# In the last layer, q's swaps asked for earlier, value products two steps later, and the q norms' scale folded into their power

## The chip, the cores and the metric

The kernel runs on one core of one Trainium2 chip. The metric is device microseconds for one execution of the whole program. A core has five engines, each with its own instruction queue: PE (TensorE, matrix products, with PEld for its weight loads), DVE (VectorE), ACT (ScalarE), POOL (GpSimd) and SP (SyncE, which here only issues DMAs). An engine runs its instructions in the order of its queue; a wait for another engine, or for a DMA, stops everything behind it in that queue.

## The reference

The program is a two-layer encoder over 272 tokens (16 learned meta tokens and 256 inputs), 2048 wide, in fp32. Each layer has an attention branch and a Fourier branch, then a gated convolution network. The part on which the change acts:

```python
proj = rmsnorm(h) @ w_in                       # q | k | v | f | ga | gf
q = rope_2d(rmsnorm(q, q_norm))                # 8 heads of 128
k = rope_2d(rmsnorm(k, k_norm))                # 2 heads, each shared by 4 q heads
p = softmax(q @ k.T / sqrt(128))
attn = p @ v
fr = Re(fft2(f over tokens and 128 channels))  # per channel group
h = h + (sigmoid(ga) * (attn @ w_attn_br) + sigmoid(gf) * (fr @ w_four)) @ w_out
```

After the second layer the meta tokens are dropped.

## The kernel before

**Products.** Every fp32 product is made from high and low parts. Weights come as chunks of 128x1024 (512 KB), loaded by SP (`load_raw`, L264) into a ring of four `raw` buffers (a few more in some stages). ACT casts a chunk to its high part (`wh`, L306), and DVE subtracts that to get the low part (`wl`, L308). Three matmuls then make one product: `wh` with the input's high part (L377), `wh` with its low part (L378), `wl` with the high part (L379). A `raw` buffer comes free when its `wl` is made, and SP issues the next load into it then, in its own order. In the last layer the products of q and of the gates are 258 columns wide, since 14 of the meta tokens are needed only as keys.

**Steps.** While such a product is under way, the smaller work of attention runs in its shadow. That work is written as generators (`kstats` for the k norm and rope, `vtrans`, `q_stage` for a pair of q heads, `attend` and `attention`, `folded_chan`), pushed onto a list with a number of steps to wait. After every second pair of weight block and output half, `group` calls `step()` (one step of the first generator that is due; `yield n` means that it waits n steps) and `pump()` (one split of the next chunk). This order of writing is what the scheduler starts from. It then orders each engine's instructions by its own estimate, except where `keep_in_program_order` or `manual_schedule` fixes them.

**Last layer.** The order is k, v, q0, q1, then `folded_f` (the Fourier product over 16 chunks of a folded weight `fw`, chunk numbers 448 to 463, whose matmuls are L869 and L872 with the high part and L873 with the low part `wl`), q2, q3, then gates (`ga`, `gf`) and branch products. q1 and `folded_f` are under `manual_schedule` for DVE, and the end of q1 and `folded_f` for ACT too.

**q_stage.** `head_evac` (L926 to L937) brings a pair of heads out of PSUM: ACT squares (L935), DVE scales (L936) into `qp`. `swap` (L946 to L950) is four DMAs on SP that exchange 32-row blocks of `qp` into `qs`, for rope. `rope` (L952 to L958) then multiplies `qs` (L953) and `qp` (L954), adds (L955), casts to the high part (ACT, L956) and subtracts to the low part (L958), all but the cast on DVE. The q norms: the sums of squares go through PE (L943) and DVE (L944, L1050, L1054), L1055 turns the 9 sums `qv` into mean plus epsilon, and POOL raises them to the power -1/2 (L518, in `pow_half`), which gives `rq`. `attention` begins by multiplying `rq` by 1/sqrt(128) on DVE (L1074).

**attention.** For each of two kv heads there are nine items: the meta tokens of four heads, then four heads by two blocks of 128 queries. An item goes through `scores` (PE L1094 to L1096 into `ps_s`; DVE maximum L1098 and bias L1100; ACT exponential L1103), `normalise` (DVE L1108 to L1112 into `pn`), `transposed` (PE L1120 into `ps_pt`; ACT L1133 writes the high part PH, DVE L1134 the low part PL and L1136). Once both blocks of a head are transposed, `values` (L1138 to L1146) makes seven matmuls into `ps_pv`: twice L1141 (PH), L1142 (PL), L1143 (PH), and one L1144. In every turn of the loop the values of the head that was finished stand behind `transposed` of a later item. PH and PL are one tile each for all four heads.

Of the kernel before, what the change touches and what calls it, by code (L numbers as in the profile page):

```python
# [13 lines left out]
ALU = mybir.AluOpType  # L14
# [9 lines left out]
HD = 128  # L24
# [5 lines left out]
EPS = 1e-6  # L30
# [131 lines left out]
def encoder_kernel(ctx, tc, xT, params, consts, bmat, cfold, csign, w_fl, w_f64c, w_in, w_abr, w_four, w_f64, w_out, w_up, w_down, w_vn, w_dn, w_dt, out):  # L162
    nc = tc.nc
# [150 lines left out]
    def push(gen, wait=0):  # L314
        shadow.append([wait, gen])
# [20 lines left out]
    def until(hold, flag):  # L336
        while flag not in hold:
            step(True)
# [174 lines left out]
    def bc2(ap):  # L513
        return _rep(ap, 2)

    def pow_half(out, src):
        n = src.shape[1]
        nc.gpsimd.tensor_tensor(out, src, mhalf[:, :n], op=ALU.pow)  # L518
# [115 lines left out]
    for l in range(DEPTH):  # L634
        last = l == DEPTH - 1
# [6 lines left out]
        with tc.tile_pool(name=f"mix{l}", bufs=1) as mp:  # L642
# [17 lines left out]
            def rt(name):  # L660
                return mp.tile([P, 2, 2 * TH], F32, tag="r", name=name, bufs=7)[:, :, :T]
# [4 lines left out]
            def ut(name):  # L666
                return mp.tile([P, T], F32, tag="u", name=name, bufs=2)
# [271 lines left out]
            def sums_t(dst, blocks):  # L939
                n = len(blocks)  # L940
                ss = psum.tile([P, 512], F32, tag="aux", name="ps_ss")
                for i in range(n):
                    nc.tensor.transpose(ss[:, i * P:(i + 1) * P], blocks[i], ident)  # L943
                nc.vector.tensor_reduce(dst, ss[:, 0:n * P].rearrange("p (i n) -> p i n", i=n), axis=AX.X, op=ALU.add)  # L944

            def swap(hp):  # L946
                qs = rt("qs")
                for b in range(4):
                    tc.keep_in_program_order(nc.sync.dma_start(qs[32 * b:32 * b + 32, :, :], hp[32 * (b ^ 1):32 * (b ^ 1) + 32, :, :]))
                return qs  # L950
# [24 lines left out]
            def kstats():  # L975
                kss = small.tile([P, 2, 3], F32, tag="kss", name="kss")
                for m in range(NKV):
                    sums_t(kss[:, m, :], (kms[m], ksq[:, m, 16:144], ksq[:, m, 144:272]))
                nc.vector.tensor_tensor(kss, kss, bc2(tok2), op=ALU.mult)
                nc.vector.tensor_scalar(kss, kss, 1.0 / HD, EPS, op0=ALU.mult, op1=ALU.add)  # L980
                rk = small.tile([P, 2, 3], F32, tag="rk", name="rk")
                pow_half(rk.rearrange("p a b -> p (a b)"), kss.rearrange("p a b -> p (a b)"))
                yield 6
                for kv in range(NKV):
                    dk = ut("dk")
                    for i, (a, b) in enumerate(BLK):
                        nc.vector.tensor_scalar(dk[:, a:b], mask[:, a:b], rk[:, kv, i:i + 1], None, op0=ALU.mult)
                    yield 5
                    pk = psum.tile([P, 512], F32, tag="aux", name="ps_kb")
                    nc.tensor.matmul(pk[:, :T], ones, dk, start=True, stop=True)  # L990
                    nc.vector.tensor_tensor(kp[:, kv, :], kp[:, kv, :], pk[:, :T], op=ALU.mult)
                yield 3
                qs = swap(kp)
                yield 8
                yield from rope(kp, qs, kH, kL)
                hold["keys"] = True

            push(kstats(), 4)
            if last:
                slots = fold_setup()  # L1000
                push(fold_ahead(slots), 2)
# [32 lines left out]
            for pn in pns:  # L1034
                nc.gpsimd.memset(pn[:, 0:P], 0.0)

            def q_stage(i, qp, qsq):
                kv, j = i // 2, i % 2
                sl = slice(2 * j, 2 * j + 2)
                if j == 0:  # L1040
                    qvs.append(small.tile([P, 9], F32, tag="qv", name="qv"))
                    qsms.append(small.tile([P, 2, 4, NM], F32, tag="sqm", name="sqm", bufs=2))
                qv, qsm = qvs[kv], qsms[kv]
                qs = swap(qp)
                yield 3
                nc.vector.tensor_copy(qsm[:, :, 2 * j:2 * j + 2, :], qsq[:, :, 0:NM].unsqueeze(1).to_broadcast([P, 2, 2, NM]))
                d4 = qv[:, 4 * j:4 * j + 4]
                sums_t(d4, [qsq[:, m, a:b] for m in range(MG) for a, b in BLK[1:]])
                d4 = d4.rearrange("p (m i) -> p m i", m=2)
                nc.vector.tensor_tensor(d4, d4, bc2(tok2[:, 1:3]), op=ALU.mult)  # L1050
                if j:
                    yield 1
                    sums_t(qv[:, 8:9], [qsm.rearrange("p r h t -> p (r h t)")])
                    nc.vector.tensor_tensor(qv[:, 8:9], qv[:, 8:9], tok2[:, 0:1], op=ALU.mult)  # L1054
                    nc.vector.tensor_scalar(qv, qv, 1.0 / HD, EPS, op0=ALU.mult, op1=ALU.add)  # L1055
                    rq = small.tile([P, 9], F32, tag="rq", name="rq")
                    pow_half(rq, qv)
                yield 6 - j
                yield from rope(qp, qs, qH[kv][:, sl, :], qL[kv][:, sl, :])
                if j:  # L1060
                    rqs.append(rq)
                    if kv == 0:
                        push(attend(), 5)
# [7 lines left out]
                    yield from attention(kv, rqs[kv])  # L1071

            def attention(kv, rq):
                nc.vector.tensor_scalar(rq, rq, 1.0 / math.sqrt(HD), None, op0=ALU.mult)  # L1074
                qm = mp.tile([P, 2, 2, 4, NM], F32R, tag="qm", name="qm")
                for j, src in enumerate((qH, qL)):
                    nc.scalar.copy(qm[:, j], src[kv][:, :, 0:NM].bitcast(F32).unsqueeze(1).to_broadcast([P, 2, 4, NM]))
# [68 lines left out]
                    nc.vector.tensor_tensor(qL[kv][:, h, lo:T], po[:, :W], qH[kv][:, h, lo:T].bitcast(F32), op=ALU.subtract)  # L1146

                items = [None] + [(h, i) for h in range(4) for i in range(2)]
                prev, ready, due = None, [], []
                for item in items + ["end", "end"]:  # L1150
                    cur = None
                    if item != "end":
                        pe, sm = scores(item)
                    yield 2
                    if item != "end":
                        cur = (item, normalise(pe, sm))
                    yield 1
                    if prev is not None:
                        transposed(*prev)
                        if prev[0] is not None and prev[0][1] == 1:  # L1160
                            due.append(prev[0][0])
                        yield 1
                    if ready:
                        values(ready.pop(0))
                    if prev is not None:
                        yield 1
                    ready, due = ready + due, []
                    prev = cur
                while ready:
                    values(ready.pop(0))  # L1170
                    yield 1

            qH, qL = [], []
            for i in range(4):
                if not (last and i == 1):
                    ps = group((l, "q", i), xr(lo), W)
                    qq = head_evac(ps, prm[:, P_QN + l:P_QN + l + 1], "qp", lo)
                if last:
                    if i in (0, 2):
                        until(hold, "vt" if i == 0 else "fold")  # L1180
                        for t_, n in ((qH, "q1"), (qL, "q2")):
                            o = Q_AT[l][t_ is qL][i // 2]
                            t = mp.tile([P, 4 * T + o], F32R, tag=n + "ab"[i // 2], name=n)
                            t_.append(t[:, o:o + 4 * T].rearrange("p (h t) -> p h t", t=T))
                elif i == 0:
                    until(hold, "vt")
                    until(hold, "fold")
                    for t_, n in ((qH, "q1"), (qL, "q2")):
                        o = Q_AT[l][t_ is qL][0]
                        t = mp.tile([P, NH * T + o], F32R, tag=n, name=n)[:, o:o + NH * T].rearrange("p (h t) -> p h t", t=T)  # L1190
                        t_ += [t[:, 0:4], t[:, 4:8]]
                if last and i == 1:
                    until(hold, "ahead")
                    with tc.manual_schedule(engines={mybir.EngineType.DVE}):
                        ps = group((l, "q", i), xr(lo), W)
                        with tc.manual_schedule(engines={mybir.EngineType.Activation}):
                            qq = head_evac(ps, prm[:, P_QN + l:P_QN + l + 1], "qp", lo)
                            folded_f(slots, E)
                    o1_tiles()
                    push(folded_chan(E), 1)  # L1200
                push(q_stage(i, *qq), 1)


            def gate(kind, i):
# [401 lines left out]
```

## Time and profile before

| | |
|---|---|
| median of 3 runs | 2517.09 us (2516.09 to 2518.9) |
| the profiled execution | 2520.21 us, with a span of 2518.4 us |
| PE busy | 2503.5 us of the span, 99% |
| DVE busy | 1988.6 us, 79% |
| ACT busy | 1339.9 us, 53% |
| POOL busy | 203.9 us, 8% |

The profiled execution is 3.1 us above the median of the others, and 1.8 us of its time lie outside the span. PE is busy nearly throughout, so a change of the small work can move the time only at the places where PE waits, or runs more slowly. In a row of the timeline stand the start and length in us, the engine, the line, the operation, `out<-in`, the shape and a count; in brackets the idle time of the engine ahead of it and what ended it.

### The profile page before, as it was taken

The page shows a single profiled execution, that of the slowest core. Times are in us where ns is not written, and L with a number is a line of the kernel's source. Part 1 is how long each engine was busy: PE and PEld are TensorE (multiplying, and loading weights), DVE is VectorE, ACT ScalarE, POOL GpSimd, SP SyncE. Part 2 cuts the span into 40 slices and gives each one's busy share as a digit, 9 for nine tenths or more (in the row PEclk, how much of TensorE's full clock was granted, in tenths as well). Part 3 has the DMA queues.
Part 4 walks back from the last instruction along what each step waited for, and adds up shares of the span by engine and source line. Part 5 has one row for each costly group of instructions (what it writes and reads, how often), then busy time and mean ns, then how long its engine had stood idle before and what let it go on. Part 6 is the DMA issues. An engine that isn't in the chain of part 4 may idle for free. (4 is left out here: it accounts for less than half of the span.)

```text
span 2518.4 us, 47932 instructions
## 1 busy us (share of the span) xinstructions
PE 2503.5 (99%) x18848; PEld 2423.2 (96%) x18848; DVE 1988.6 (79%) x3159; ACT 1339.9 (53%) x1913; POOL 203.9 (8%) x394
## 2 busy tenths in 40 slices
PE   9999999999999999999999999999999999999999
PEld 9999999999999999999999999999988899999987
DVE  7687866778878677888768877666879787898898
ACT  6455534454444334444445555444676665666665
POOL 0000000012212222222200000000000000000000
PEclk9999999999999999999999999999999999999999
DMA  7444557879999999999975547888888887788887
GB/s 248 166 156 163 188 198 245 261 267 378 396 335 378 407 384 374 397 381 379 400 268 177 193 141 224 272 262 261 259 260 293 298 289 241 260 282 290 280 301 272
DMA packets 194802, 706.85 MB, mean 281 GB/s; under 512 B 22144, under 2 KB 27392, under 8 KB 194320
## 3 DMA queue, kind: packets, MB, share of 16 engines
q1 hardware_dynamic: 146768, 517.09, 58.4%
q0 software_dynamic: 46368, 184.57, 21.1%
q8 instruction: 147, 2.41, 0.4%
q10 hardware_dynamic: 1440, 2.13, 0.2%
q14 instruction: 79, 0.65, 0.1%
HBM read 623.32 MB, written 111.15 MB: 292 GB/s over the span
## 5 line engine op out<-in xcount | busy, mean ns | idle before, releaser
L306 ACT CAST wh<-raw 128x1024 fp32r<-128x1024 f32 (+1 forms) x961 | 998.6, 1044 | 888.9 <-PE ps_ug L378 190.2
L308 DVE TENSOR_TENSOR wl<-raw,wh 128x1024 fp32r<-128x1024 f32 (+1 forms) x961 | 1159.2, 1218 | 391.0 <-ACT wh L306 378.1
L377 PE MATMUL ps_ug<-xHL,wh 128*128 128x272 f32 (+1 forms) x1408 | 401.1, 285 | 0.0
L379 PE MATMUL ps_ug<-xHL,wl 128*128 128x272 f32 (+1 forms) x1408 | 399.4, 285 | 0.0
L378 PE MATMUL ps_ug<-xHL,wh 128*128 128x272 f32 (+1 forms) x1408 | 399.1, 284 | 0.0
L377 PEld LDWEIGHTS ps_ug<-xHL,wh 128*128 128x128 f32 x1408 | 265.4, 188 | 3.2
L378 PEld LDWEIGHTS ps_ug<-xHL,wh 128*128 128x128 f32 x1408 | 265.0, 188 | 3.2
L379 PEld LDWEIGHTS ps_ug<-xHL,wl 128*128 128x128 f32 x1408 | 264.7, 188 | 1.1 <-DVE wl L308 0.4
L1446 PE MATMUL ps_p<-wh,opnd 128*128 128x512 f32 x816 | 222.3, 393 | 0.0
L379 PE MATMUL ps_uv<-xHL,wl 128*128 128x272 f32 x704 | 202.2, 287 | 0.0
L379 PE MATMUL ps_d<-gHL,wl 128*128 128x272 f32 x704 | 202.1, 287 | 0.0
L377 PE MATMUL ps_uv<-xHL,wh 128*128 128x272 f32 x704 | 201.7, 286 | 0.0
L377 PE MATMUL ps_d<-gHL,wh 128*128 128x272 f32 x704 | 201.5, 286 | 0.0
L378 PE MATMUL ps_uv<-xHL,wh 128*128 128x272 f32 x704 | 201.0, 285 | 0.0
L378 PE MATMUL ps_d<-gHL,wh 128*128 128x272 f32 x704 | 201.0, 285 | 0.0
L1446 PEld LDWEIGHTS ps_p<-wh,opnd 128*128 128x128 f32 x816 | 148.5, 188 | 28.5 <-ACT wh L306 0.2
L377 PE MATMUL ps_ga<-xHL,wh 128*128 128x272 f32 (+1 forms) x512 | 148.6, 290 | 0.0
L377 PE MATMUL ps_gf<-xHL,wh 128*128 128x272 f32 (+1 forms) x512 | 147.0, 287 | 0.0
L540 DVE TENSOR_TENSOR wi<-wi,wi 128x512 f32<-128x512 f32 x224 | 146.9, 685 | 0.0
L378 PE MATMUL ps_ga<-xHL,wh 128*128 128x272 f32 (+1 forms) x512 | 146.2, 286 | 0.0
L379 PE MATMUL ps_ga<-xHL,wl 128*128 128x272 f32 (+1 forms) x512 | 146.2, 286 | 0.0
L379 PE MATMUL ps_o<-mH,wl 128*128 128x272 f32 (+1 forms) x512 | 146.0, 285 | 0.0
(380 smaller groups left out, 5974.0 us busy)
## 6 DMA issues: line engine op xcount, KB each, us to landing
raw<-in_w_up SPq DMA_DIRECT2D x288, 512.0 KB, 6.4
raw<-in_w_in SPq DMA_DIRECT2D x191, 512.0 KB, 4.2
raw<-in_w_down SPq DMA_DIRECT2D x88, 512.0 KB, 7.3
wi<-in_w_dn POOLq DMA_DIRECT2D x80, 512.0 KB, 9.3
ft<-wi POOLq DMA_DIRECT2D x80, 512.0 KB, 7.7
raw<-ft SPq DMA_DIRECT2D x80, 512.0 KB, 4.7
raw<-in_w_out SPq DMA_DIRECT2D x64, 512.0 KB, 4.2
raw<-fv SPq DMA_DIRECT2D x64, 512.0 KB, 4.8
```

Source lines behind the costliest of these rows:

```text
L306: nc.scalar.copy(h[:, a:b], r[:, a:b])
L308: nc.vector.tensor_tensor(lo[:, a:b], r[:, a:b], h[:, a:b].bitcast(F32), op=ALU.subtract)
L377: nc.tensor.matmul(o, h[:, c, sl], a, start=kt == 0, stop=False)
L378: nc.tensor.matmul(o, h[:, c, sl], b, start=False, stop=False)
L379: nc.tensor.matmul(o, lo[:, c, sl], a, start=False, stop=kt == nk - 1)
L540: tt = lambda *v, **kw: tc.keep_in_program_order(nc.vector.tensor_tensor(*v, **kw))
L1446: nc.tensor.matmul(ps[h], x, w[:, 512 * h:512 * h + 512], start=fresh and (s_, q) in BEGIN and first, stop=(s_, q) in END and end, skip_gr ...
```

## The change

Four edits. In the last layer `kstats` starts after 6 steps instead of 4 and then pauses for 4 instead of 6, so its statistics are two steps later and what follows is where it was. In the last layer `swap(qp)` is written when `q_stage` is pushed, and not at its first step. In both layers L1055 no longer divides by 128 but adds 128 times epsilon, so that the power gives rq/sqrt(128) at once, and L1074 goes. In the last layer a finished head's values are held until after the scores of the next turn, between two steps.

```diff
@@ kstats
-                yield 6
+                yield 4 if last else 6
-            push(kstats(), 4)
+            push(kstats(), 6 if last else 4)
@@ q_stage
-            def q_stage(i, qp, qsq):
+            def q_stage(i, qp, qsq, qs=None):
-                qs = swap(qp)
+                if qs is None:
+                    qs = swap(qp)
                 yield 3
...
-                    nc.vector.tensor_scalar(qv, qv, 1.0 / HD, EPS, op0=ALU.mult, op1=ALU.add)
+                    nc.vector.tensor_scalar(qv, qv, EPS * HD, None, op0=ALU.add)
                     rq = small.tile([P, 9], F32, tag="rq", name="rq")
                     pow_half(rq, qv)
@@ attention
-                nc.vector.tensor_scalar(rq, rq, 1.0 / math.sqrt(HD), None, op0=ALU.mult)
...
-                prev, ready, due = None, [], []
+                prev, held, ready, due = None, [], [], []
                 for item in items + ["end", "end"]:
                     cur = None
                     if item != "end":
                         pe, sm = scores(item)
-                    yield 2
+                    if held:
+                        yield 1
+                        values(held.pop(0))
+                        yield 1
+                    else:
+                        yield 2
...
-                    if ready:
+                    if ready and not last:
                         values(ready.pop(0))
                     if prev is not None:
                         yield 1
-                    ready, due = ready + due, []
+                    if last:
+                        held, ready, due = held + ready, due, []
+                    else:
+                        ready, due = ready + due, []
                     prev = cur
+                ready = held + ready
                 while ready:
@@ the loop over q
-                push(q_stage(i, *qq), 1)
+                push(q_stage(i, *qq, swap(qq[0]) if last else None), 1)
```

In the new code the lines from L1045 to L1073 are one further down, those from there to L1148 where they were, and those behind `attention` nine further down.

The instructions change places between the k statistics and the end of attention in the last layer; elsewhere only L1074 is missing. The first place is DVE ahead of `folded_f`. Names carry a buffer number; `wl446` is the low part of chunk 446, `kp` and `qp` are k and the first q pair. Before:

```order
L936 SCALAR_TENSOR_TENSOR qp_16728<-ps_1_q_0_0_16553,prm_72,rstdB_81 128x258
L953 TENSOR_TENSOR qs_16640<-qs_16640,cst_73 128x2x272
L954 TENSOR_TENSOR kp_16362<-kp_16362,cst_73 128x2x272
L936 SCALAR_TENSOR_TENSOR qp_16728<-ps_1_q_0_1_16554,prm_72,rstdB_81 128x258
L955 TENSOR_TENSOR kp_16362<-kp_16362,qs_16640 128x2x272
L308 TENSOR_TENSOR wl446_16758<-raw446_16555,wh446_16757 128x4x256
```

Now:

```order
L936 SCALAR_TENSOR_TENSOR qp_16726<-ps_1_q_0_0_16551,prm_72,rstdB_81 128x258
L953 TENSOR_TENSOR qs_16638<-qs_16638,cst_73 128x2x272
L954 TENSOR_TENSOR kp_16360<-kp_16360,cst_73 128x2x272
L308 TENSOR_TENSOR wl446_16756<-raw446_16553,wh446_16755 128x4x256
L955 TENSOR_TENSOR kp_16360<-kp_16360,qs_16638 128x2x272
L936 SCALAR_TENSOR_TENSOR qp_16726<-ps_1_q_0_1_16552,prm_72,rstdB_81 128x258
```

`wl446` now stands ahead of the add of k's rope and of the second half of `qp`, which were ahead of it.

SP at the same place, its queue before; `fw` is the folded weight, and the first swap here is k's:

```order
L949 DMA qs_16640<-kp_16362 32x2x272 x4
L264 DMA raw448_16653<-fw_66 128x1024
L264 DMA raw449_16693<-fw_66 128x1024
L264 DMA raw450_16742<-fw_66 128x1024
L949 DMA qs_16752<-qp_16728 32x2x272 x4
L264 DMA raw451_16787<-fw_66 128x1024
```

And now:

```order
L949 DMA qs_16638<-kp_16360 32x2x272 x4
L264 DMA raw448_16651<-fw_66 128x1024
L264 DMA raw449_16691<-fw_66 128x1024
L258 DMA r64_18921<-in_w_f64 64x256
L264 DMA raw450_16745<-fw_66 128x1024
L949 DMA qs_16736<-qp_16726 32x2x272 x4
L264 DMA raw451_16785<-fw_66 128x1024
```

q0's swap still stands behind the load of chunk 450; a small load for a branch weight (`r64`) has come in ahead of it.

PE at the start of chunk 449 in `folded_f`, where its low part is first used, before (`ps_f` are the eight sums, `hA` the folded input):

```order
L869 MATMUL ps_f00_16892<-hA_16372,wh449_16860 128x276
L872 MATMUL ps_f00_16892<-hA_16372,w64s_16213 16x138 x2
L869 MATMUL ps_f01_16893<-hA_16372,wh449_16860 128x276
L869 MATMUL ps_f10_16894<-hA_16372,wh449_16860 128x276
L869 MATMUL ps_f11_16895<-hA_16372,wh449_16860 128x276
L869 MATMUL ps_f20_16896<-hA_16372,wh449_16860 128x276
L873 MATMUL ps_f00_16892<-hA_16372,wl449_16861 128x138
```

Now:

```order
L869 MATMUL ps_f00_16890<-hA_16370,wh449_16858 128x276
L872 MATMUL ps_f00_16890<-hA_16370,w64s_16211 16x138 x2
L873 MATMUL ps_f00_16890<-hA_16370,wl449_16859 128x138
L869 MATMUL ps_f01_16891<-hA_16370,wh449_16858 128x276
L873 MATMUL ps_f01_16891<-hA_16370,wl449_16859 128x138
```

Four matmuls with `wh449` that stood ahead of the first use of `wl449` now stand behind it.

PE at the end of the first head's value product in the last layer, before (`ga` is a gate's product):

```order
L1141 MATMUL ps_pv_18097<-PH_17791,VH_16218 128x258
L377 MATMUL ps_1_ga_1_0_18011<-xHL_71,wh477_17965 128x258
L378 MATMUL ps_1_ga_1_0_18011<-xHL_71,wh477_17965 128x258
L379 MATMUL ps_1_ga_1_0_18011<-xHL_71,wl477_17966 128x258
L377 MATMUL ps_1_ga_1_1_18012<-xHL_71,wh477_17965 128x258
L378 MATMUL ps_1_ga_1_1_18012<-xHL_71,wh477_17965 128x258
L379 MATMUL ps_1_ga_1_1_18012<-xHL_71,wl477_17966 128x258
L1094 MATMUL ps_s_18113<-kH_16216,q1_16736 128x272
L1095 MATMUL ps_s_18113<-kL_16217,q1_16736 128x272
L1096 MATMUL ps_s_18113<-kH_16216,q2_16737 128x272
L377 MATMUL ps_1_ga_1_0_18011<-xHL_71,wh478_18028 128x258
L1142 MATMUL ps_pv_18097<-PL_17792,VH_16218 128x258
```

Now:

```order
L1096 MATMUL ps_s_18100<-kH_16214,q2_16735 128x272
L377 MATMUL ps_1_ga_1_0_18008<-xHL_71,wh478_18025 128x258
L378 MATMUL ps_1_ga_1_0_18008<-xHL_71,wh478_18025 128x258
L379 MATMUL ps_1_ga_1_0_18008<-xHL_71,wl478_18026 128x258
L377 MATMUL ps_1_ga_1_1_18009<-xHL_71,wh478_18025 128x258
L378 MATMUL ps_1_ga_1_1_18009<-xHL_71,wh478_18025 128x258
L379 MATMUL ps_1_ga_1_1_18009<-xHL_71,wl478_18026 128x258
L1141 MATMUL ps_pv_18119<-PH_17793,VH_16216 128x258
L1142 MATMUL ps_pv_18119<-PL_17794,VH_16216 128x258
L1143 MATMUL ps_pv_18119<-PH_17793,VL_16217 128x258
L1141 MATMUL ps_pv_18119<-PH_17793,VH_16216 128x258
L1142 MATMUL ps_pv_18119<-PL_17794,VH_16216 128x258
```

The head's seven matmuls stood in two pieces, four and three, around six matmuls of the gate and the next scores; now they stand together behind those. The fifth of them, the second L1142, is five matmuls further down.

## The prediction

> **What bounds the kernel.** I read the page first, then PE's waits, then the granted clock around each of them, and last the engines that end those waits. The page shows span and busy time:
>
> ```profile
> span 2518.4 us, 47932 instructions
> PE 2503.5 (99%) x18848; PEld 2423.2 (96%) x18848; DVE 1988.6 (79%) x3159; ACT 1339.9 (53%) x1913; POOL 203.9 (8%) x394
> ```
>
> PE is the bound. The change leaves its work alone, so it can gain or lose only at PE's stops and in what they do to the clock. The view of waits for PE (total us, times, longest) is short:
>
> ```profile
> PE ps_f L444 <- ACT wh L306: 4.8, 2, 4.5
> PE ps_pv L1142 <- DVE PL L1134: 2.9, 3, 1.8
> PE ps_f L873 <- DVE wl L308: 2.7, 1, 2.7
> PE ps_ss L943 <- DVE sqm L972: 0.4, 1, 0.4
> PE ps_uv L374 <- DVE wl L308: 0.3, 1, 0.3
> ```
>
> L444 is the program's start and L374 the feed-forward part, both untouched. The second, third and fourth row are the change's three places, 6.0 us in all. The windows around the two longest of these waits show that they cost more than their length (columns: busy us of PE, PEld, DVE, ACT, POOL with counts, then granted clock, DMA share, GB/s):
>
> ```profile
> core 0: us, PE busy (x) PEld busy (x) DVE busy (x) ACT busy (x) POOL busy (x), PEclk, DMA share, GB/s
> 1366.60:1369.40 2.80, 0.10 (x1) 0.00 (x0) 2.14 (x5) 0.65 (x1) 0.00 (x0) 1.00 0.01 4
> 1370.00:1376.70 6.70, 6.70 (x33) 6.53 (x33) 5.22 (x8) 3.38 (x6) 0.00 (x0) 0.50 0.69 235
> 1376.80:1380.00 3.20, 3.20 (x30) 3.17 (x29) 2.05 (x4) 1.66 (x2) 0.00 (x0) 1.00 0.60 183
> 1460.90:1462.00 1.10, 1.10 (x9) 1.10 (x10) 1.04 (x4) 0.46 (x2) 0.00 (x0) 1.00 0.42 134
> 1462.10:1465.20 3.10, 3.10 (x17) 3.10 (x15) 2.20 (x6) 0.67 (x2) 0.00 (x0) 0.50 0.41 139
> 1465.30:1468.00 2.70, 2.70 (x24) 2.70 (x24) 1.62 (x3) 1.45 (x2) 0.00 (x0) 0.97 0.39 149
> 1531.00:1538.00 7.00, 7.00 (x60) 7.00 (x61) 6.45 (x14) 4.73 (x11) 1.34 (x2) 1.00 0.28 87
> ```
>
> After the stop at 1366.7 PE runs 6.8 us at a clock of 0.50, after the one at 1459.1 some 3.2 us. Half rate loses half of that: 3.4 and 1.6 us. After the third, shorter stop (0.92 us, row below) the clock stays 1.00.
>
> **Part 1, the start of the folded product (swap and kstats).** The rows in order of time:
>
> ```profile
> 1355.72 0.48 DVE L936 SCALAR_TENSOR_TENSOR qp<-ps_q,prm,rstdB 128x258 f32<-128x258 f32 x1
> 1356.11 0.72 DVE L955 TENSOR_TENSOR kp<-kp,qs 128x544 f32<-128x544 f32 x1
> 1356.74 1.22 DVE L308 TENSOR_TENSOR wl<-raw,wh 128x1024 fp32r<-128x1024 f32 x1
> 1358.03 0.32 SPq L264 DMA_DIRECT2D raw<-fw  x1
> 1358.45 2.56 SPq L949 DMA_DIRECT2D qs<-qp  x4
> 1359.42 2.36 DVE L308 TENSOR_TENSOR wl<-raw,wh 128x1024 fp32r<-128x1024 f32 x2
> 1364.62 0.73 DVE L953 TENSOR_TENSOR qs<-qs,cst 128x544 f32<-128x544 f32 x1 [2.84 <-DMA qs<-qp]
> 1365.98 0.72 PE L869 MATMUL ps_f<-hA,wh 128*128 128x276 f32 x4
> 1367.50 0.73 DVE L958 TENSOR_TENSOR q<-qp,q 128x544 fp32r<-128x544 f32 x1 [0.66 <-ACT q L956]
> 1368.14 1.22 DVE L308 TENSOR_TENSOR wl<-raw,wh 128x1024 fp32r<-128x1024 f32 x1
> 1369.41 0.93 PE L873 MATMUL ps_f<-hA,wl 128*128 128x138 f32 x5 [2.72 <-DVE wl L308]
> ```
>
> PE waits for wl449, which stands on DVE behind q0's rope. The rope waits 2.84 us for q0's swap, which was issued behind the load of chunk 450. That load waited for a free buffer, which came when wl446 ended at 1357.96. So the swap was late because wl446 was late, and the source order of the swap alone doesn't matter: it still stands behind chunk 450. What changes is DVE's order. With wl446 ahead of L955 it starts at about 1355.7 and ends at 1356.9. The second L936, now behind both, then becomes the bound: 1355.7 + 1.2 + 0.7 + 0.4 = 1358.0, and the swaps start there in place of 1358.45, 0.4 earlier. The add of k's rope, later by 1.2 us, delays only kL, which has until attention.
>
> How long the swap takes is open. The two later DMAs of the four, and all swaps:
>
> ```profile
> L949 SPq DMA_DIRECT2D qs<-qp x2: 595/612/629, 1359.7 to 1360.4; - x2
> DMA to landing us min/median/max: 2.4/3.2/4.0
> DMA to landing us min/median/max: 2.1/2.8/4.7
> ```
>
> The last, issued at 1360.4, took 4.0 us, against a median of 2.8 over all. Chunk 450 was issued 0.4 us ahead of the swaps. It now goes 1.0 ahead, so less of it is left to share the DMA engines with; for that I take 2.4, the shorter of the two in this group. Then rope starts at 1364.62 - 0.4 - 1.6 = 1362.6. From there to PE's resumption is a chain of fixed work (1369.41 - 1364.62 = 4.8), so PE resumes at 1367.4: -2.0. Against that, PE stops earlier: of the five L869 that filled the time ahead of the wait, four (0.72 us) now stand behind it: +0.7. The stop is then 2.7 - 2.0 + 0.7 = 1.4 us. Does half rate follow? 0.92 brought none, 1.79 did. The two stretches begin 92.1 us apart, 27 times 3.41, and last two and one such pieces, so I read the clock as judged piece by piece. In the piece ending at 1369.93, PE was idle 2.72 of 3.41 us (80%), in the one ending at 1462.06 1.79 (52%). At most 41% fits in one now, and a boundary may cut it further. I take it as gone: -3.4. Part 1 by this: -2.0 + 0.7 - 3.4 = -4.7. If the swap again takes 4.0, -0.4 + 0.7 = +0.3, and half rate stays.
>
> In this part also: ACT's cast for q's rope goes ahead of wh450, which isn't needed until some 20 matmuls after the resumption, and the loads of `folded_chan`'s constants go behind q1's swap; PE meets none of these in its waits, so I put them at nothing. With that cover gone each costs at most a cast, 1 us. The later k statistics end the wait at L943 (0.4 us): the matmul stands 12 matmuls further down, 12 x 7.00/60 = 1.4 us. -0.4.
>
> **Part 2, L1074 and the held values.**
>
> ```profile
> L1074 DVE TENSOR_SCALAR rq<-rq x4: 174/174/175, 123.2 to 1449.7; 128x9 f32<-128x9 f32 x4
>   POOL rq L518: 7.3, 4
> 1449.72 0.17 DVE L1074 TENSOR_SCALAR rq<-rq 128x9 f32<-128x9 f32 x1 [1.91 <-POOL rq L518]
> 1448.20 1.04 ACT L306 CAST wh<-raw 128x1024 fp32r<-128x1024 f32 x1
> 1450.43 1.21 DVE L308 TENSOR_TENSOR wl<-raw,wh 128x1024 fp32r<-128x1024 f32 x1
> 1460.39 0.41 DVE L1134 TENSOR_TENSOR PL<-ps_pt,PH 128x256 fp32r<-128x256 f32 x1
> 1460.85 0.39 PE L1142 MATMUL ps_pv<-PL,VH 128*128 128x258 f32 x1 [1.79 <-DVE PL L1134]
> 1511.92 0.39 PE L1142 MATMUL ps_pv<-PL,VH 128*128 128x258 f32 x1 [0.21 <-DVE PL L1134]
> 1530.89 0.39 PE L1142 MATMUL ps_pv<-PL,VH 128*128 128x258 f32 x1 [0.92 <-DVE PL L1134]
> ```
>
> L1074 is a trifle itself, but DVE stands 1.91 us in front of it for POOL's power each time. In layer 0 and for the first kv head PE has no wait behind it: nothing gained. The fourth, at 1449.72, is followed by DVE work without a gap up to the PL at 1460.39 that PE waits for. Up to 2.1 us (1.91 + 0.17) could be won; but wl477 (1450.43) needs its cast from ACT, done at 1449.24, so 1.2 is what passes. PL then ends at 1459.6. Holding the values puts L1142 five matmuls (0.6 us) further down. 1.79 - 1.2 - 0.6 = 0.0; I take 0.1 of stop, with 0.6 the other end, should half of DVE's gain be lost to PE's own pace. The later heads' L1142 move by 10 to 19 matmuls, 1.2 us and more, past their 0.21 and 0.92. So -2.8 of 2.9, and the half rate of 1.6 goes: -4.4. L1055 with one operation in place of two I put at nothing: it stands in the same place and PE isn't waiting.
>
> **Sum.** Against the profiled execution's own 2520.2 (span 2518.4 and 1.8 around it): -4.7 - 0.4 - 4.4 = -9.5, 2510.7. The median shown is 2517.1, 3.1 lower, which would fit runs in which one of the half-rate stretches is shorter, so not all of 5.0 may be there to win; off the median the sum would give 2507.6. I forecast 2510, nearer the end that has a trace.
>
> **Rivals.**
> - *The swap lands late again.* Four us happened with DMA traffic that is much the same. Then part 1 is +0.3, and the sum -4.5: 2515.7 off the profiled execution, 2512.6 off the median. Within 0.2%, mostly.
> - *The half rate isn't the waits'.* Both stretches begin 0.5 to 1.2 us after a stop, which speaks for the waits; that there are two cases only speaks against. Then only idle goes: -1.3 - 0.4 - 2.8 = -4.5, 2515.7 or 2512.6. The Trainium skill ("TensorE: Matmul & The Clock Gate", section "Why this matters for your kernels") asks for no idle gaps above about 3 us; by that neither stop would have dropped the clock and this rival would be the forecast. The trace disagrees: 1.79 us of idle was followed by 0.50.
> - *A wait takes its place (slower).* The held `ps_pv` now takes its PSUM buffer between `ps_s` and `ps_pt`, from the ring of four that these share. If each of the eight heads' turns thereby stops PE, it costs 8 x the stop; from 1.2 us each it eats the 9.5. With stops like the first head's (1.79 and 1.6 of half rate) it is 8 x 3.4 = 27 us less the 9.5, 2535 off the median. For it speaks how tight these chains run:
>
> ```profile
> 1443.31 0.24 DVE L1112 TENSOR_SCALAR pn<-pe,rs 128x48 f32<-128x48 f32 x1
> 1443.54 0.52 PE L1120 MATMUL ps_pt<-cst,pn 128*128 128x128 f32 x3
> ```
>
> DVE ends the tile that PE transposes at 1443.55, when the transposes begin, and these now stand three matmuls earlier. Against it: no wait of PE for a PSUM buffer is in the view of waits.
>
> **Chances.** The forecast 0.52, the late swap 0.25, the clock 0.08, the new wait 0.15. A measurement of this kernel can tell some 0.2% (5 us) from no change, so faster is below 2512.1, slower above 2522.1. Faster: 0.9 of the first, a fifth of the second, a tenth of the third: 0.53. Slower: most of the last and a sliver of the second: 0.13. The rest, 0.34, is within. The range holds the first three, from the sum off the median less 1.6 (2506) to the late swap's 2515.7 with 0.8 for a stop of 0.6 in part 2 and some noise: 2516.5.
>
> **What would show it.** In the changed kernel's waits L1142 is gone or below 0.5 in all, L943 is gone, L873 is near 1.4. No window near 1370 or 1460 has a clock of 0.50. On DVE the wait in front of q0's L953 is about 1 us. Wrong would be: a wait of 2 us or more still at L873, a new row for `ps_s`, `ps_pt` or `ps_pv`, or 0.50 after a stop of about 1 us.

## The result, and the profile after

The changed kernel takes 2510.97 us, the median of 14 runs (2509.1 to 2515.67), against 2516.99 us for the kernel before beside it (14 runs, 2514.68 to 2522.0). The ratio is 0.9977, with a 95% interval of 0.9970 to 0.9984: 0.2% faster. The profiled execution took 2510.57 us, with a span of 2508.5.

The view of PE's waits after the change (total us, times, longest):

```profile
PE ps_f L444 <- ACT wh L306: 6.0, 2, 4.4
PE ps_f L873 <- DVE wl L308: 1.1, 1, 1.1
PE ps_pv L1142 <- DVE PL L1134: 0.6, 1, 0.6
PE ps_uv L374 <- DVE wl L308: 0.3, 1, 0.3
```

Of the 6.0 us at the three places 1.7 are left: L943 is gone, L873 waits 1.1 us in place of 2.7, L1142 0.6 in place of 2.9. The first row is the program's start, which the change leaves alone: it was 4.8 us before, and lies between 4.6 and 6.2 in the profiles of this study. The windows that had a granted clock of 0.50 are at 1.00 now (columns as in the prediction):

```profile
1367.30:1370.00 2.70, 2.70 (x23) 2.67 (x24) 1.97 (x4) 0.69 (x1) 0.00 (x0) 1.00 0.54 196
1370.00:1376.70 6.70, 6.67 (x58) 6.38 (x57) 6.23 (x9) 4.79 (x8) 0.00 (x0) 1.00 0.68 230
1459.00:1466.00 7.00, 7.00 (x61) 7.00 (x60) 6.11 (x16) 3.63 (x8) 0.00 (x0) 1.00 0.34 125
```

PE does 58 matmuls in the 6.7 us after 1370.0, where it did 33 before. At the start of the folded product, the timeline of DVE, SP and PE, and then the landing times of the swap's four DMAs:

```profile
1355.86 1.22 DVE L308 TENSOR_TENSOR wl<-raw,wh 128x1024 fp32r<-128x1024 f32 x1
1357.63 0.48 DVE L936 SCALAR_TENSOR_TENSOR qp<-ps_q,prm,rstdB 128x258 f32<-128x258 f32 x1
1358.26 2.52 SPq L949 DMA_DIRECT2D qs<-qp  x4
1362.49 0.73 DVE L953 TENSOR_TENSOR qs<-qs,cst 128x544 f32<-128x544 f32 x1 [0.57 <-DMA qs<-qp]
1367.30 0.33 PE L873 MATMUL ps_f<-hA,wl 128*128 128x138 f32 x1 [1.09 <-DVE wl L308]
```

```profile
DMA to landing us min/median/max: 2.1/2.2/2.5
```

Chunk 446's low part (first row) is ahead of the second half of `qp`, the swap is 0.2 us earlier, and its slowest DMA takes 2.5 us in place of 4.0. At the value products:

```profile
1454.45 0.41 DVE L1134 TENSOR_TENSOR PL<-ps_pt,PH 128x256 fp32r<-128x256 f32 x1
1454.69 0.28 PE L1141 MATMUL ps_pv<-PH,VH 128*128 128x258 f32 x1
1454.91 0.39 PE L1142 MATMUL ps_pv<-PL,VH 128*128 128x258 f32 x1
1522.15 0.39 PE L1142 MATMUL ps_pv<-PL,VH 128*128 128x258 f32 x1 [0.61 <-DVE PL L1134]
```

The first head's L1142 follows the L1141 ahead of it by 0.22 us, where other pairs are 0.12 apart: 0.1 us of stop is left of 1.79. The 0.6 us in the waits are all at a later head, where there were 0.92.

Not every run is like the profiled one. In 17 of the changed kernel's 24 runs (all of this study) the mean granted clock is 1.0, and their median is 2510.0 us; in 7 it is 0.998 or 0.999, with 2515.3. For the kernel before, 15 of the 66 runs whose clock is listed have 1.0, with a median of 2514.8, and 51 less, with 2517.6. The experiments look for the reason.

### The profile page after: what moved, and what is told of

It reads as the page before. It is cut to its first block, busy times and chain, and to the rows that moved or that the text cites. A ratio compares the mean times of both kernels' runs of the same rounds, so it can differ in the third digit from the quotient of the medians.

```text
span 2508.5 us, 47931 instructions
## 1 busy us (share of the span) xinstructions
PE 2496.9 (100%) x18848; PEld 2416.3 (96%) x18848; DVE 1987.7 (79%) x3155; ACT 1341.0 (53%) x1913; POOL 205.4 (8%) x394
## 4 chain that ended last, share of the span: by engine, by line
PE 98%; DVE 1%; DMA 1%; issue 0%; POOL 0%; ACT 0%; ACTq 0%; DVEq 0%; POOLq 0%
PE ps_p L1455 14%; PE ps_ug L379 7%; PE ps_ug L377 7%; PE ps_ug L378 7%; PE ps_d L379 3%; PE ps_uv L379 3%; PE ps_uv L377 3%; PE ps_uv L378 3%; PE ps_d L377 3%; PE ps_d L378 3%; PE ps_ga L377 2%; PE ps_o L379 2%; PE ps_o L377 2%; PE ps_ga L378 2%; PE ps_ga L379 2%; PE ps_gf L377 2%
## 5 line engine op out<-in xcount | busy, mean ns | idle before, releaser
L377 PE MATMUL ps_o<-mH,wh 128*128 128x272 f32 (+1 forms) x512 | 145.5, 284 | 0.0
```

What stands on the lines that cost most here:

```text
L377: nc.tensor.matmul(o, h[:, c, sl], a, start=kt == 0, stop=False)
```

## The experiments

The theory is the prediction's: the change takes idle time of PE away at L873 and L1142, and with the long stops the half rate that follows them. The rivals: the swap's landing decides, whatever the order; the low clock has another cause; new waits.

### Each part alone

The later k statistics alone:

```diff
-                yield 6
+                yield 4 if last else 6
-            push(kstats(), 4)
+            push(kstats(), 6 if last else 4)
```

> The kernel before with the later k statistics alone. Theory (the late chunk 446 was what made q0's swap late): DVE's order around chunk 446 becomes that of the changed kernel, so PE's wait at L873 falls from 2.7 to about 1.1 us, no window near 1370 us has a clock of 0.50, the wait at L943 is gone, and L1142 keeps its 2.9 us. Some 5 us faster than before. Rival (the swap's earlier place in the source is what counts): L873 keeps 2.7 us or more and half rate; only the 0.4 us at L943 goes, and the time is within 1 us of before.

2514.39 us (11 runs), ratio 0.9992 (0.9983 to 1.0001). Its profiled execution:

```profile
PE ps_pv L1142 <- DVE PL L1134: 2.6, 3, 1.8
PE ps_f L873 <- DVE wl L308: 1.0, 1, 1.0
```

L943 is gone, L873 at 1.0 and L1142 as before, as the theory has it. In time it is 2.7 us by the medians, with an interval that just reaches 1, and not 5: only 3 of its 11 runs had a clock of 1.0 (2513.65), the others 2515.9.

q's swaps written earlier, alone:

```diff
-                qs = swap(qp)
+                if qs is None:
+                    qs = swap(qp)
-                push(q_stage(i, *qq), 1)
+                push(q_stage(i, *qq, swap(qq[0]) if last else None), 1)
```

> The kernel before with q's swaps written earlier, alone. Theory: the swap still stands behind the load of chunk 450, which still waits for chunk 446 on DVE, so it is issued at the same 1358.4 us. L873 waits 2.7 to 3.4 us (four matmuls that filled the wait now stand behind it), half rate stays: 0 to 0.7 us slower than before. Rival (the earlier place counts): L873 falls to about 1 us, the half rate goes, 5 us faster.

2512.96 us (11 runs), ratio 0.9980 (0.9971 to 0.9990). The expectation was wrong: it took SP's order from the changed kernel, and here SP has the swap ahead of chunk 450:

```order
L264 DMA raw449_16693<-fw_66 128x1024
L949 DMA qs_16738<-qp_16728 32x2x272 x4
L264 DMA raw450_16747<-fw_66 128x1024
L264 DMA raw451_16787<-fw_66 128x1024
L264 DMA raw452_16817<-fw_66 128x1024
```

The timeline of SP and DVE, the landing of the swap's DMAs, and PE's waits (lines behind the edit are one further down in this kernel: L1143 for L1142):

```profile
1356.13 2.52 SPq L949 DMA_DIRECT2D qs<-qp  x4
1361.48 0.72 DVE L953 TENSOR_TENSOR qs<-qs,cst 128x544 f32<-128x544 f32 x1
```

```profile
DMA to landing us min/median/max: 2.1/2.1/2.1
```

```profile
PE ps_pv L1143 <- DVE PL L1135: 2.5, 3, 1.7
PE ps_f L873 <- DVE wl L308: 0.4, 1, 0.4
```

The swap is issued as soon as `qp` is there, DVE doesn't wait for it at all, and PE waits 0.4 us. All 11 runs have a clock of 1.0, and lie between 2512.4 and 2514.3. So the edit does what its words say, when it is made alone.

The scale in the power, alone (both L1055 and L1074):

```diff
-                    nc.vector.tensor_scalar(qv, qv, 1.0 / HD, EPS, op0=ALU.mult, op1=ALU.add)
+                    nc.vector.tensor_scalar(qv, qv, EPS * HD, None, op0=ALU.add)
-                nc.vector.tensor_scalar(rq, rq, 1.0 / math.sqrt(HD), None, op0=ALU.mult)
```

> The kernel before with the norm's scale in the power, and L1074 gone, alone. Theory: DVE no longer stands 1.9 us at 1449.7 us, its low part PL comes 1.2 us earlier, and the first wait at L1142 falls from 1.8 to about 0.6 us; no half rate near 1462. The waits of 0.2 and 0.9 us at the later heads stay. 1.2 + 1.6 = 2.8 us faster. Rival (the held values alone matter): the first wait keeps 1.5 us or more, time as before.

2515.62 us (11 runs), ratio 0.9995 (0.9986 to 1.0004). Its waits (behind L1074 the lines are one up here, L1141 for L1142), and the timeline at its first stop at the value products:

```profile
PE ps_f L873 <- DVE wl L308: 2.9, 1, 2.9
PE ps_pv L1141 <- DVE PL L1133: 1.4, 3, 0.6
```

```profile
1458.27 0.39 PE L1141 MATMUL ps_pv<-PL,VH 128*128 128x258 f32 x1 [0.53 <-DVE PL L1133]
```

The first stop went from 1.79 to 0.53 us, 1.26 less where 1.2 was expected, and no half rate follows it. The time moved by 1.5 us by the medians and can't be told from no change.

The held values, alone (of which these lines are the core):

```diff
-                    yield 2
+                    if held:
+                        yield 1
+                        values(held.pop(0))
+                        yield 1
+                    else:
+                        yield 2
...
-                    if ready:
+                    if ready and not last:
                         values(ready.pop(0))
...
+                    if last:
+                        held, ready, due = held + ready, due, []
```

> The kernel before with the values held two steps longer, alone. Theory: the first L1142 stands five matmuls further down, so its wait falls from 1.8 to 1.2 us; the later waits of 0.2 and 0.9 us are gone: 1.7 us of idle less. A stop of 1.2 us fills 35% of a piece of 3.41 us, which is between what brought half rate (52%) and what didn't (27%). So 1.7 us faster, or 3.3 with the half rate gone. Rival (scores, transposes and values now wait for one another's PSUM buffers): new waits at L1094 or L1120, 5 us slower or more.

2513.64 us (11 runs), ratio 0.9981 (0.9972 to 0.9990). PE's waits and, in the timeline, its two longest stops at the value products:

```profile
PE ps_pv L1142 <- DVE PL L1134: 1.8, 2, 1.1
PE ps_f L873 <- DVE wl L308: 1.4, 1, 1.4
```

```profile
1455.78 0.39 PE L1142 MATMUL ps_pv<-PL,VH 128*128 128x258 f32 x1 [1.15 <-DVE PL L1134]
1523.07 0.39 PE L1142 MATMUL ps_pv<-PL,VH 128*128 128x258 f32 x1 [0.61 <-DVE PL L1134]
```

The first stop is 1.15 us, as expected, and the one of 0.21 is gone, but one of 0.61 remains at the later head. There is no new wait: the slower rival falls. And L873 waits 1.4 us here, though nothing was changed ahead of it; in the kernel with the scale alone it was 2.9. The swap's landing, 3.4 us for the slowest DMA here and 4.2 there, differs from run to run with the same order.

### The parts against each other

The changed kernel without the edit of the k statistics:

```diff
-                yield 4 if last else 6
+                yield 6
-            push(kstats(), 6 if last else 4)
+            push(kstats(), 4)
```

> The changed kernel with the k statistics where they were. In the run of the swap edit alone the swap went ahead of chunk 450 and L873 waited 0.4 us. Theory: the same here: L873 0.4 us, L943 0.4 us back, L1142 0.6 us as in the changed kernel: idle of PE 0.3 us less in all, about 2509.8 us, and no run above 2512 with a clock below 1.0, since no stop is longer than 0.6 us. Rival (the low clock in some runs of the changed kernel comes from the stop at L1142): still a third of the runs at 2514 us and more.

2509.48 us (5 runs, 2508.9 to 2510.2), ratio 0.9964 (0.9950 to 0.9978), all five with a clock of 1.0.

```profile
PE ps_ss L943 <- DVE sqm L972: 0.7, 1, 0.7
PE ps_pv L1142 <- DVE PL L1134: 0.6, 1, 0.6
PE ps_f L873 <- DVE wl L308: 0.4, 1, 0.4
```

The swap goes ahead of chunk 450 and L873 falls to 0.4, as expected; the price, L943, is 0.7 rather than 0.4 us. The rival, that the low clock comes from L1142's stop, finds nothing in these five runs. Five runs alone could be chance: with the changed kernel's share of 17 in 24, five of five would come up about one time in six. Together with the swap alone and the last kernel of this part, which also have the swap ahead of chunk 450, it is 21 runs of 21.

The changed kernel without the edit of the swap:

```diff
-                if qs is None:
-                    qs = swap(qp)
+                qs = swap(qp)
-                push(q_stage(i, *qq, swap(qq[0]) if last else None), 1)
+                push(q_stage(i, *qq), 1)
```

> The changed kernel with q's swaps where they were. In both, q0's swap stands behind chunk 450 on SP, so if the later k statistics alone decide where chunk 446 goes on DVE, this is the changed kernel: L873 1.1 us, L1142 0.6, L943 none, 2510 us in runs with a clock of 1.0. Rival (in the changed kernel the swap's earlier place does some of the work): L873 1.5 us or more, and 2511 us.

2510.04 us (10 runs), ratio 0.9982 (0.9967 to 0.9997), 2509.95 in the eight runs with a clock of 1.0 (the two others are at 2516.6 and 2525.0). L873 waits 1.3 us and L1142 (here L1141, the lines being one up) 0.6:

```profile
PE ps_f L873 <- DVE wl L308: 1.3, 1, 1.3
PE ps_pv L1141 <- DVE PL L1133: 0.6, 1, 0.6
```

So in the changed kernel the swap's edit does nothing that can be seen. The likely reason, from the orders: with the later k statistics chunk 446 ends sooner, and chunk 450, free to go sooner, is put ahead of the swap again. Of the two edits for the same place the one undoes the other's work.

The changed kernel without the edit of the k statistics, and with q0's rope three steps later, so that wl449 comes ahead of its low part:

```diff
-                yield 6 - j
+                yield 6 - j + (3 if last and i == 0 else 0)
```

> The changed kernel with the k statistics where they were, and q0's rope pausing three steps more before it begins, so that wl449 stands ahead of the low part of q0 (L958) on DVE. Theory: the 0.4 us at L873 is gone too (1.4 us of DVE work and waiting no longer stand ahead of wl449): 2509.4 us, steady. Rival (q0's later low part, or a cast of ACT that now waits, is missed later): a new wait of PE after 1370 us, and a time above the kernel without the k statistics' edit alone.

2510.39 us (5 runs, 2509.5 to 2511.3), ratio 0.9968 (0.9956 to 0.9981). The waits show what was meant, L873 gone and nothing new, with L943 gone too:

```profile
PE ps_f L444 <- ACT wh L306: 5.3, 2, 4.5
PE ps_pv L1142 <- DVE PL L1134: 0.6, 1, 0.6
```

Its profiled span, 2507.4, is the lowest of the profiled ones, but its five runs aren't below those of the kernel without the k statistics' edit alone: their median is 0.9 us above, where the theory had 0.4 below a forecast of 2509.8. What is left to gain there is under what five runs can tell.

### Where the low clock comes from

The changed kernel with wl449 delayed on DVE:

```diff
                 yield from rope(qp, qs, qH[kv][:, sl, :], qL[kv][:, sl, :])
+                if last and i == 0:
+                    for _ in range(2):
+                        nc.vector.tensor_tensor(qL[kv][:, sl, :], qp, qH[kv][:, sl, :].bitcast(F32), op=ALU.subtract)
```

> The changed kernel with q0's low part computed three times over on DVE (twice more, the same result), which delays wl449 by 1.3 to 1.6 us. Theory (half rate follows a long stop): L873 waits 2.4 to 2.7 us, and most runs show a clock below 1.0 and lie 1.5 + 1.7 to 1.5 + 3.4 us above the changed kernel's best, that is 2512.7 to 2514.4; runs without half rate at 2511. Rival (the clock has another cause): only 1.5 us more than the changed kernel in every run, and as many runs with a low clock as it has.

2513.39 us (11 runs, 2511.1 to 2518.2), ratio 0.9986 (0.9977 to 0.9995). 9 of the 11 runs have a clock below 1.0, median 2514.0; the two with 1.0 are at 2511.1 and 2512.2. The stop, and the windows around it:

```profile
1367.63 0.48 PE L873 MATMUL ps_f<-hA,wl 128*128 128x138 f32 x1 [2.68 <-DVE wl L308]
```

```profile
1365.00:1366.70 1.70, 0.00 (x0) 0.00 (x0) 1.67 (x4) 0.38 (x1) 0.00 (x0) 1.00 0.00 0
1366.90:1373.50 6.60, 5.87 (x27) 5.79 (x28) 3.83 (x6) 1.99 (x2) 0.00 (x0) 0.50 0.47 160
```

A stop made longer brings the half rate, as the theory has it, and here the clock falls at 1366.8, while PE still stands. The rival that the clock has another cause is out. Three of the nine runs lie at 2517.1 to 2518.2 us, above the 2514.4 that the theory allowed; they have no profile, so what more they lose is open.

The changed kernel again, beside these:

> The changed kernel once more, on the same chip as the three beside it. Theory: two groups of runs, at 2509 to 2511 us with a clock of 1.0 and some at 2514 to 2516 with 0.998 or 0.999; waits at L873 of 1.1 and at L1142 of 0.6 us. If the profiled run is one of the second group, its windows show where the half rate lies: after L873 by the theory, after L1142 by the rival.

2510.0 us (9 runs), ratio 0.9969 (0.9956 to 0.9981): eight runs at 2509.9 with a clock of 1.0, one at 2516.2 with 0.998. The profiled one was of the first kind. A further profiled execution was of the second kind, at 2515.48 us:

> The changed kernel, for a look at one of its runs with a low clock, which are about a quarter of them: if this is one, half rate follows L873 and the swap lands late there (a wait of 2 us or more, by the theory that only long stops count), or follows the wait of 1.1 us (then shorter stops do it too).

Its waits, the timeline and the landing of the swap, and the windows after the stop at L873:

```profile
PE ps_f L873 <- DVE wl L308: 3.3, 1, 3.3
PE ps_pv L1142 <- DVE PL L1134: 0.6, 1, 0.6
```

```profile
1359.06 2.52 SPq L949 DMA_DIRECT2D qs<-qp  x4
1365.11 0.73 DVE L953 TENSOR_TENSOR qs<-qs,cst 128x544 f32<-128x544 f32 x1 [2.39 <-DMA qs<-qp]
```

```profile
DMA to landing us min/median/max: 2.1/2.3/3.9
```

```profile
1369.40:1376.10 6.70, 6.19 (x28) 6.10 (x29) 4.04 (x7) 1.99 (x2) 0.00 (x0) 0.50 0.47 158
1376.30:1380.00 3.70, 3.70 (x35) 3.64 (x34) 3.63 (x7) 2.66 (x5) 0.00 (x0) 1.00 0.56 174
```

That is the prediction's first rival in a run of the changed kernel: the same order on SP, with the load of chunk 450 issued 1.15 us ahead of the swap in both, but the slowest swap DMA takes 3.9 us in place of 2.5. By the packets in the traces it is a few that are late: 252 of the swap's 256 begin within 3.7 us of its issue, as all do in the quick execution, and the last four 4.6 to 4.9 us after it. L953 waits 2.39 us, PE 3.3, and half rate follows for 6.8 us. 2.2 us more of idle (3.3 against 1.1) and 6.2 us of busy PE at half rate, which lose 3.1, are 5.3 of the 5.5 us by which this run lies above 2510.0.

Two more profiled executions of the later k statistics alone:

> The later k statistics alone again, for a look at where the clock falls: 8 of its 11 runs had a clock of 0.999, its profiled run 1.0. It stops 1.0 us at L873 and 1.8 us at L1142. By the pieces of 3.41 us half rate should follow the stop at L1142 (52% of a piece) and not that at L873 (30%). Rival: after L873, as the swap alone stops 0.4 us there and 1.7 at L1142, and had a clock of 1.0 in all 11 runs.

> As the run before it, for a second look: half rate after 1460 us by the pieces, after 1367 us by the rival, or none in this run.

In both the swap landed late, 3.5 and 4.0 us for the slowest, and again it is four packets that come behind the rest. The first (2518.91 us) stopped 2.86 us at L873 and 1.78 at L1142, and half rate followed each, for one piece:

```profile
1371.40:1374.60 3.20, 3.20 (x17) 3.12 (x17) 2.05 (x3) 1.99 (x2) 0.00 (x0) 0.50 0.71 251
1460.10:1463.40 3.30, 3.30 (x17) 3.30 (x17) 3.06 (x9) 1.05 (x3) 0.00 (x0) 0.50 0.53 164
```

The second (2517.88 us) stopped 3.39 us at L873, with half rate from 1367.9 to 1374.8, and 1.73 us at L1142, with none. Neither the expectation nor its rival had seen that L873's wait is not 1.0 us in such runs.

## Why the prediction was right or wrong

The forecast was 2510 us with a range of 2506 to 2516.5; it is 2511.0. By its steps:

- **Part 1, chunk 446 ahead of the second `qp`: right in the profiled execution, and partly by luck.** PE resumes after 1.09 us of stop where 1.4 was worked out, L953 waits 0.57 us where about 1 was, the slowest swap DMA takes 2.5 where 2.4 was taken. But of the 2.1 us by which PE resumes earlier, the swap's earlier issue gives only 0.2, and most of the rest is its landing, 2.5 us in place of 4.0. The prediction's reason for that, that less of chunk 450 is left to share the DMA engines with, doesn't settle it: with the load the same 1.15 us ahead the landing is 2.4 to 2.7 us in five profiles and 3.5 to 4.0 in three. The kernel without the swap's edit, at the same time, confirms that here the source order of the swap doesn't matter. But the reason given, that the swap stands behind chunk 450 anyway, holds only beside the later k statistics: alone, the swap's edit works, and better. The order was read for the whole change and taken to hold for its parts.
- **Half rate after L873: gone, but not in every run.** The chance of 0.25 for a late swap was set for the kernel as a whole; what came is a share of runs: 7 of 24 have a low clock, and the one of them that was profiled has the late swap. That 7 of 24 is near 0.25 is chance. The median is a run with a clock of 1.0.
- **L943: gone**, as said. The later k statistics are worth that (0.4 to 0.7 us), and cost about as much at L873 (1.1 against 0.4) and the steadiness.
- **Part 2: the first head right, a later head wrong.** Of 1.79 us 0.1 is left, as worked out; the scale alone took off 1.26 where 1.2 was expected, holding alone 0.64 where 0.6 was. The step that failed is "the later heads' L1142 move by 10 to 19 matmuls, past their 0.21 and 0.92": 0.61 is left of 0.92. Even that difference isn't the change's. In the five further profiles with the values where they were (k statistics alone three times, swap alone, scale alone) this stop is 0.63 or 0.64 us, and in all eight with the values held it is 0.61; the 0.92 belongs to one execution. The row of the k statistics alone:

```profile
1524.39 0.39 PE L1142 MATMUL ps_pv<-PL,VH 128*128 128x258 f32 x1 [0.63 <-DVE PL L1134]
```

So holding wins 0.02 us there, and of the later heads' waits only the 0.21 is gone. The waiting matmul moved, but so did PL. In the profile after, DVE makes a whole chunk's low part ahead of that head's normalisation, and ACT its cast ahead of the exponential; with the k statistics alone DVE made it earlier, at 1520.13, ahead of that head's maximum. That this order is what delays PL is read from the rows, and no run tests it:

```profile
1518.84 1.05 ACT L306 CAST wh<-raw 128x1024 fp32r<-128x1024 f32 x1 [2.16 <-issue]
1519.79 0.58 ACT L1103 ACTIVATE pe<-ps_s,nb,rq 128x272 f32<-128x272 f32 x1
1519.92 1.23 DVE L308 TENSOR_TENSOR wl<-raw,wh 128x1024 fp32r<-128x1024 f32 x1 [0.27 <-ACT wh L306]
1521.69 0.41 DVE L1134 TENSOR_TENSOR PL<-ps_pt,PH 128x256 fp32r<-128x256 f32 x1
```

- **The sum: right between the two profiled executions, too much on the clock for the median.** From 2520.2 to 2510.6 us these differ by 9.6, where 9.5 was worked out. Runs with a clock of 1.0 went from 2514.8 to 2510.0: 4.8 us, where the idle terms come to 4.5; no run of the kernel before with 1.0 has a profile, so whether those stop as long as the profiled one isn't known. The 5.0 us of half rate were those of one execution; over the runs before, the 51 with less than 1.0 lie only 2.8 us above the 15 with it (2517.6 against 2514.8). The medians differ by 6.0 and not by 9.5. So it is partly luck that the forecast lies within 1 us of the median: it starts from an execution 3.1 us above the median before, and takes off 3.5 us more than the medians lost.
- **The rivals.** The late swap happens, in a share of the runs, as said. With the load of chunk 450 ahead of it, its landing decides the stop at L873 (1.0 to 1.4 us, or 2.7 to 3.4 when it is late); with the swap ahead of the load, 0.4 us or nothing is left. The new wait on PSUM buffers shows in no profile. The clock's other cause falls with the delayed wl449. The rule of the Trainium skill ("TensorE: Matmul & The Clock Gate", section "Why this matters for your kernels"), no idle above about 3 us, is contradicted again: a stop of 1.78 us brought a clock of 0.50.

## What to carry to other kernels

A change that moves small work is priced at the stops of the bounding engine, and each stop with the half rate that follows it; both come from single executions, so the spread of the runs has to be read before a stop's price is added to a median. Where a change has two edits for the same place, read the order of each alone as well: here one undid the other, and without it the kernel is as fast at the median, with all its five runs at a clock of 1.0. A small transfer on the critical path, here q0's swap, has a landing time that varies by up to 1.6 us between executions with the same order, so a landing read from one execution is no price for an order; issuing it earlier than the large loads took that out here.

## What the runs showed of the hardware

- **Half rate goes in pieces.** All the stretches seen last 3.4 or 6.8 us, and two in the same run begin 92.1 us (27 pieces of 3.41) or 88.7 us (26) apart. The pieces lie differently in each run.
- **Which stops bring it.** Of the profiled stops, those up to 1.4 us (0.92, 1.09, 1.10, 1.15, 1.26, 1.4) brought none; 1.78, 1.79, 2.68, 2.72, 2.86, 2.9, 3.30 and 3.39 did; 1.69, 1.73 and 1.77 didn't. Counted piece by piece, in steps of 3.41 us from a change of the clock in the same trace, it becomes clearer. Around these stops, a piece at full rate in which PE was idle for 52, 53, 54, 62, 68, 80 or 80% was followed by half rate; one with 50 or 51% was not, nor was any with less, but for one. The piece with the stop at L1142 in the swap alone, in the k statistics alone, and in the first of its two further executions (columns as in the prediction):

```profile
1452.00:1455.41 3.41, 1.72 (x14) 1.50 (x14) 3.38 (x9) 2.32 (x6) 0.00 (x0) 1.00 0.43 154
1452.70:1456.11 3.41, 1.68 (x14) 1.46 (x13) 3.38 (x8) 2.35 (x6) 0.00 (x0) 1.00 0.45 154
1456.63:1460.04 3.41, 1.63 (x14) 1.41 (x13) 3.38 (x9) 2.24 (x6) 0.00 (x0) 1.00 0.45 154
```

  Only the third was followed by 0.50. So about half a piece of idle time is enough here, and the 1.69 us of the swap alone stay just under it, which fits its 11 runs with a clock of 1.0. A boundary between two pieces can save a stop: the 1.73 us were cut into 1.38 and 0.35. The one case that doesn't fit is the stop of 2.86 us, cut into 1.32 and 1.54 (39 and 45% of a piece), after which half rate came all the same.
- **The landing of a 68 KB DMA varies.** With the load of chunk 450 issued 1.15 us ahead of the four, the slowest took 2.4 to 2.7 us in five profiles and 3.5 to 4.0 in three; with the load 0.42 us ahead, as in the kernel before, 3.4 to 4.2 in three; with the swap ahead of the load, 2.1 in each of three. In the five slowest of these, four of the swap's 256 packets begin 0.5 us or more behind all others. In the late run of the changed kernel chunk 451's load follows the swap on the same queue, as in the quick ones, so what holds these packets up is not shown.
